# One GpSimd pass for the small inverses of two sequence mixers, with their matrix products planned together

## The chip, the cores and the metric

The kernel runs on one core of one Trainium2 chip. The metric is the device time of one launch in microseconds (us), the median of several runs; lower is better. A profiled execution of the same program gives a trace: every instruction of every engine with its start and duration. The engines are the matrix engine (TensorE, called PE in the profile), two elementwise engines (VectorE = DVE, ScalarE = ACT), GpSimd (POOL) and SyncE (SP), which here only issues DMA transfers.

## What is computed

One layer of a streaming encoder on a sequence of 512 tokens of width 2048, in float32:

```python
xn = rmsnorm(x); y = xn @ W_in               # 59 column blocks of 128
h  = x + concat[GDN(y_gdn), RWKV7(y_rwkv)] @ W_out
h  = h + cross_attention(rmsnorm(h), rmsnorm(mem))
h  = h + relu(rmsnorm(h) @ W_up)**2 @ W_down
out = rmsnorm(h)
```

GDN is a gated delta rule with 8 heads of 128, RWKV7 a state-space recurrence with 16 heads of 64. Both are causal recurrences that the kernel computes chunk by chunk. In both, each chunk of 64 tokens needs the inverse of a 64x64 triangular matrix (in the reference: `triangular_solve` in GDN, the step-by-step scan in RWKV7).

## The kernel before

**Stages.** (1) The input projection and both mixers run together: the 59 blocks of `y` are computed one after the other, and beside them, in 8 rounds, one RWKV column block (two heads of 64) and one GDN head per round. Block 3+7j to 9+7j belong to round j, in the order r, k, v of RWKV and k, q, v, z of GDN. (2) The keys of the attention (`kp`, `kq`), its values (`vp`, `vo`), the output projection (`op`), the scores (`sc`), the attention output (`at`). (3) The MLP: up in 32 units, down in 8, both by Strassen's seven products. Large products are done in fp32r, as three products of a split operand (`whi`, `wlo`, `xhi`, `xlo`); the small products of the mixers are plain fp32, which the trace shows as two passes each.

**Who sets the order.** Stage 1 is written as generators ("chains", L279 to 318), each yielding one instruction after the other. A planner inside the kernel (`run`, `start`, `cost`, `issue`, L211 to 318) keeps a modelled clock of each engine, and issues next the instruction that could start first. On TensorE equal starts go by rank: the mixers' chains (rank 3) ahead of the projections (rank 4). [...] So a mixer's small product runs as soon as the planner thinks its inputs ready, and the stream of `py` products fills all the rest. `cost` charges 100 ns for a change to another small tile shape and 120 ns for the first fp32r product after an fp32 one.

**A round of RWKV** (`rwkv`, L858 to 1081): decay (`pW`, `pA`, two Tanh, a scan, two Exp), key, normalisation, then the Gram matrices `GA`, `GB` by `pgA`, `pgB`; transposes and value products (`pk`, `pat`, `pv`, `pak`, `pkv`); the inverse; two levels that grow the 16x16 inverses to 64x64 (tiles `ri<j>x/w/s/t/u`); `pu`, `pwt`; eight state steps of two small products each (`rs`); the output (`po`, `pp`), its normalisation, and the store. The next round's chain starts after `pu`, `pwt` (L1029).

**A round of GDN** (`gdn`, L1092 to 1237): convolution and normalisation of the key, `pkk`, the masked matrix `NTm`; then the inverse, and beside it convolution of q and v, `pqk`, `pkt`, `pvt`; two levels (`gi<j>...`, six steps of small products); four state steps (`gs`), the output `gpo`, normalisation and store. The next round's chain starts at the very end (L1237).

**The inverses** (`inverse_blocks`, L767 to 806): the 64x64 matrices go to a DRAM tile (`nd`), come back as their 16x16 diagonal blocks, one block per partition; GpSimd runs 15 steps of two instructions on them; the result (T and its transpose U) goes through DRAM (`bg`) into the tiles where the levels read it. RWKV has 64 blocks a round, GDN 32; each has its own pass, and a list `solving` keeps the two passes from overlapping. Six loads bring T and U back for each mixer, issued on SP.

**Weight sums.** Strassen's products of the MLP's down weights need four sums of weight blocks per group (13 groups). Chains of low rank compute them on VectorE wherever there is room (`presum`, L400): four loads into `ds`, four subtractions or additions, four stores to DRAM (`sd`). What is not done in stage 1 is done during the MLP (`remaining`).

**The scores** (L1694 to 1727) are written without the planner: per step a load of 1024 columns, a split, 24 products.

## Time and profile before

| | us |
|---|---|
| median of 3 runs | 2889.58 |
| lowest and highest run | 2887.1, 2890.51 |
| span of the profiled execution | 2890.0 |
| TensorE busy, share of the span | 2862.2, 99% |
| VectorE busy | 2333.9, 81% |
| ScalarE busy | 1571.7, 54% |
| GpSimd busy | 214.7, 7% |
| stage 1 with the attention keys | 0 to about 1118 |

The span is the time from the first to the last instruction of that one execution. In the views of the trace a row of the timeline gives start, duration and the tiles (output<-inputs) of an instruction or of a run of like ones; the ends of matrix products are modelled, since they are pipelined, so the distance between two starts says more than a duration.

### The profile page before, as it was taken

How to read it: one execution, taken by the hardware profiler on the slowest of the kernel's cores; microseconds unless marked ns; L12 is line 12 of the kernel's file. 1: busy time of each engine (PE TensorE's matmuls, PEld its weight loads, DVE VectorE, ACT ScalarE, POOL GpSimd, SP SyncE). 2: the span in 40 equal slices, each digit the busy share in tenths (PEclk: the TensorE clock that was granted, in tenths of full speed). 3: DMA queues.
4: the chain of work that ended last, by engine and by line, in shares of the span. 5: the costliest groups of instructions: out<-in, count | busy, mean ns of one | idle time of the engine just before them, and what ended most of it. 6: DMA issues, size and time to landing. Idle time of an engine off the chain costs nothing.

```text
span 2890.0 us, 49168 instructions
## 1 busy us (share of the span) xinstructions
PE 2862.2 (99%) x18794; PEld 2419.1 (84%) x18794; DVE 2333.9 (81%) x3559; ACT 1571.7 (54%) x2233; POOL 214.7 (7%) x539
## 2 busy tenths in 40 slices
PE   9999999999999999999999999999999999999998
PEld 7877887877877888889988888888888888888887
DVE  7787787787877877769956898899998878786888
ACT  6555555645656655664445556555555644454544
POOL 0213213213212100000000000000000000000000
PEclk9999999999999999999999999999999999999999
DMA  5656656657656788784422354666565878887733
GB/s 191 166 147 176 176 149 187 165 154 189 180 161 200 214 257 274 232 292 151 124 95 88 110 164 153 199 195 207 189 200 178 292 249 277 295 257 247 265 101 110
DMA packets 321212, 553.01 MB, mean 191 GB/s; under 512 B 101128, under 2 KB 188428, under 8 KB 320976
## 3 DMA queue, kind: packets, MB, share of 16 engines
q1 hardware_dynamic: 293584, 518.41, 58.7%
q10 hardware_dynamic: 27392, 31.46, 3.1%
q8 instruction: 147, 2.41, 0.3%
q14 instruction: 89, 0.73, 0.1%
HBM read 443.45 MB, written 106.31 MB: 190 GB/s over the span
## 4 chain that ended last, share of the span: by engine, by line
PE 94%; DMA 3%; DVE 1%; ACT 1%; issue 1%; ACTq 0%; SPq 0%; DVEq 0%
PE py L257 22%; PE mxu L257 12%; PE mgd L257 6%; PE mgu L257 6%; PE mxd L257 6%; PE op L122 6%; PE vp L122 3%; PE mmu L257 3%; PE sc L122 3%; PE at L122 3%; PE scrd L257 3%; PE scgd L257 3%; PE mmd L257 3%; PE kq L257 3%; PE kp L257 2%; DMA wraw<-in_wo 1%
## 5 line engine op out<-in xcount | busy, mean ns | idle before, releaser
L257 ACT CAST whi<-wraw 128x1024 fp32r<-128x1024 f32 (+1 forms) x365 | 382.8, 1049 | 370.1 <-PE py L257 138.7
L257 DVE TENSOR_TENSOR wlo<-wraw,whi 128x1024 fp32r<-128x1024 f32 (+1 forms) x365 | 446.8, 1224 | 90.0 <-ACT whi L257 82.5
L257 PE MATMUL py<-xhi,whi 128*128 128x512 f32 x928 | 373.9, 403 | 6.8 <-ACT xhi L257 6.8
L257 PE MATMUL py<-xhi,wlo 128*128 128x512 f32 x928 | 373.1, 402 | 0.0
L257 PE MATMUL py<-xlo,whi 128*128 128x512 f32 x928 | 372.4, 401 | 0.0
L257 ACT CAST whi<-w 128x1024 fp32r<-128x1024 f32 x178 | 187.6, 1054 | 174.0 <-PE scgd L257 42.3
L257 DVE TENSOR_TENSOR wlo<-w,whi 128x1024 fp32r<-128x1024 f32 x178 | 217.3, 1221 | 43.4 <-ACT whi L257 40.9
L257 PE MATMUL mxu<-cb,whi 128*128 128x512 f32 x1016 | 249.3, 392 | 0.0
L257 PEld LDWEIGHTS mxu<-cb,whi 128*128 128x128 f32 x1016 | 184.7, 189 | 34.3
L257 PEld LDWEIGHTS py<-xhi,whi 128*128 128x128 f32 x928 | 175.3, 189 | 42.0 <-ACT xhi L257 6.8
L257 PEld LDWEIGHTS py<-xhi,wlo 128*128 128x128 f32 x928 | 175.3, 189 | 34.7 <-issue 1.0
L257 PEld LDWEIGHTS py<-xlo,whi 128*128 128x128 f32 x928 | 175.3, 189 | 33.8 <-DVE xlo L257 0.5
L131 DVE TENSOR_TENSOR wlo<-wraw,whi 128x1024 fp32r<-128x1024 f32 x112 | 136.7, 1222 | 44.8 <-ACT whi L130 44.3
L130 ACT CAST whi<-wraw 128x1024 fp32r<-128x1024 f32 x112 | 117.6, 1051 | 86.8 <-PE op L122 26.2
L257 PE MATMUL mxu<-cb,wlo 128*128 128x256 f32 x1016 | 142.7, 283 | 0.7 <-DVE wlo L257 0.7
L257 PEld LDWEIGHTS mxu<-cb,wlo 128*128 128x128 f32 x1016 | 135.1, 191 | 6.0 <-DVE wlo L257 0.9
L257 PE MATMUL mgu<-cb,whi 128*128 128x512 f32 x512 | 129.3, 394 | 0.1
L257 PE MATMUL mxd<-whi,cb 128*128 128x512 f32 x512 | 126.8, 389 | 0.0
L257 PE MATMUL mgd<-whi,cb 128*128 128x512 f32 x512 | 126.4, 389 | 0.0
L257 ACT ACT_TABLE_LOAD x87 | 111.6, 1283 | 16.5 <-DVE suml_gon L257 8.6
L122 PE MATMUL op<-ob,whi 128*128 128x256 f32 (+1 forms) x752 | 115.2, 304 | 0.0
L257 ACT CAST whi<-ws 128x1024 fp32r<-128x1024 f32 x75 | 79.0, 1053 | 64.0 <-PE mgu L257 48.1
(943 smaller groups left out, 6429.3 us busy)
## 6 DMA issues: line engine op xcount, KB each, us to landing
wraw<-in_w_in SPq DMA_DIRECT2D x116, 512.0 KB, 4.7
wraw<-in_w_up SPq DMA_DIRECT2D x65, 512.0 KB, 3.6
w<-in_w_up SPq DMA_DIRECT2D x63, 512.0 KB, 4.2
ds<-in_w_dm SPq DMA_DIRECT2D x128, 205.0 KB, 4.4
sd_s<-ds SPq DMA_DIRECT2D x128, 205.0 KB, 4.9
wraw<-sd_s SPq DMA_DIRECT2D x51, 512.0 KB, 4.9
w<-sd_s SPq DMA_DIRECT2D x50, 512.0 KB, 5.5
w<-in_w_dm SPq DMA_DIRECT2D x48, 512.0 KB, 4.9
```

What stands on the lines that cost most here:

```text
L122: PE.matmul(o, l, r, start=start, stop=stop, skip_group_check=again)
L130: S.copy(hi, src)
L131: V.tensor_tensor(out=lo, in0=src, in1=hi.bitcast(F32), op=ALU.subtract)
L257: f(*a, **k)
```

## The change

1. One pass on GpSimd per round for the blocks of both mixers: partitions 0 to 63 RWKV, 64 to 95 GDN. It starts when both matrices are stored. The writes of T and U of both come first, then RWKV's six loads, then GDN's six.
2. The planner adds 200 ns (`LEAVE`) to the start of an fp32r product while TensorE stands in fp32, so that another small product which could start within 200 ns goes first. It charges 190 ns instead of 100 for a change to another small shape, and 230 instead of 120 for the first fp32r product after a shape of fewer than 128 rows.
3. The decay part of RWKV's next round becomes a chain of its own (`decay`), released in the middle of the round before ("room"), and it must be drawn before the levels start. The key part of GDN becomes a chain of its own (`keys`), started after the inverse of the round before. GDN's next chain starts before the output's normalisation instead of after the store.
4. Some tiles take turns (`E2`/`v`, `tA`/`tB`), the scan is done in two halves with a shorter constant, GDN's state moves to another tile.
5. In the scores, every even step loads four blocks of down weights (512 columns) and every odd step sums and stores them: 8 pieces, two groups.
6. In the down projection's last unit one buffer is given back only after the sum that reads it.

The core of the diff:

```diff
-    CROSS = 150.0
+    CROSS, LEAVE = 150.0, 200.0
@@ cost
-                return n * 0.417 + (13.3 if state["shape"] is None else 120.0)
+                return n * 0.417 + (13.3 if state["shape"] is None else 120.0 if state["shape"][0] == P else 230.0)
-            sw = 0 if state["shape"] == sh or sh == (128, 128) else 100
+            sw = 0 if state["shape"] == sh or sh == (128, 128) else 190
@@ run
                 t = max(start(o) for o in c[3])
+                if c[3][0][0] == "PE" and state["shape"] is not None and c[3][0][6][0].dtype == F32R:
+                    t += LEAVE
@@ inverse_blocks
-    def inverse_blocks(nm, store, m, tags, temps, ready, out, moved=False):
-        np_ = 4 * m
...
-        yield lambda: not solving
-        solving.append(nm)
+    def inverse_blocks(j, tags, outs):
+        yield after("keys", j)
+        s1, s2 = tl("sgi"), tl("sgj", 240)
+        np_ = 96
...
-        yield SY.dma_start(D, blk)
+        rows_ = {"r": (slice(0, 64), 16), "g": (slice(64, 96), 8)}
+        for x in "rg":
+            yield after("stored", f"{x}i{j}")
+            yield SY.dma_start(D[rows_[x][0]], blks[f"{x}i{j}"])
...
+        for x in "rg":
+            r, m = rows_[x]
+            for t, b in (("T", Td), ("U", Ud)):
+                yield SY.dma_start(views(bg[m, t])[1], b[r])
+        for x in "rg":
+            r, m = rows_[x]
+            if x == "g":
+                yield after("gq", j)
...
+            events.add((f"{x}i", j))
@@ rwkv
+    def decay(j):
...
+        if j:
+            yield after("room", j)
         pW, pA = psb(f"pW{j}"), psb(f"pA{j}")
...
+        events.add(("drawn", j))
...
+        for s in (slice(0, 256), slice(256, 512)):
+            yield DV.tensor_tensor_scan(out=E2[:, s], data0=K("rst64"), data1=E2[:, s], initial=0.0,
+                                        op0=ALU.mult, op1=ALU.add)
...
+        events.add(("head", j))
+    def rwkv(j):
+        yield after("head", j)
+        tA, E1, E2 = heads.pop(j)
+        if j < 7:
+            chain(decay(j + 1), 3)
...
+        chain(stored(f"ri{j}", 16, store), 1)
+        chain(inverse_blocks(j, {"r": ("r", tE(j)), "g": ("gk", "gqn")}, outs), 1)
...
+        events.add(("room", j + 1))
...
         yield after("ri", j)
+        if j < 7:
+            yield after("drawn", j + 1)
@@ gdn
+    def keys(h):
...
+        fronts[h] = E, EG, eg, kn
+        events.add(("keys", h))
...
         events.add(("inverted", h))
-        vns, Ss = tl("gEs"), tl("gEG")
+        vns, Ss = tl("gEs"), tl("gqn")
+        if h < 7:
+            chain(keys(h + 1), 3)
...
+        if h < 7:
+            chain(gdn(h + 1), 3)
         o = tl("gkt")
...
-        if h < 7:
-            chain(gdn(h + 1), 3)
@@ scores
+    def fetched():
+        e, m, c, n = spans.pop(0)
...
+        for i in (A21, A22, A11, A12):
+            nc.sync.dma_start(b[i], I["w_dm"][e, m][i][:, c:n])
+    def summed():
+        e, m, c, n, (a11, a21, a22, a12) = held.pop()
+        for j, o, x, y, op in (("s1", a22, a21, a22, ALU.add), ("s3", a21, a11, a21, ALU.subtract),
+                               ("s2", a11, a22, a11, ALU.subtract), ("s4", a12, a12, a11, ALU.subtract)):
+            V.tensor_tensor(out=o, in0=x, in1=y, op=op)
+            nc.sync.dma_start(Sd[e, m, j][:, c:n], o)
...
             split(raw, wh, wl)
+            if n2 % 2 == 0:
+                fetched()
+            else:
+                summed()
```

## The prediction

> **What bounds the kernel now.** I read the page first, then who waits on the matrix engine, then its timeline inside one round, then the queues beside it. The page:

> ```profile
> span 2890.0 us, 49168 instructions
> PE 2862.2 (99%) x18794; PEld 2419.1 (84%) x18794; DVE 2333.9 (81%) x3559; ACT 1571.7 (54%) x2233; POOL 214.7 (7%) x539
> PEclk9999999999999999999999999999999999999999
> PE 94%; DMA 3%; DVE 1%; ACT 1%; issue 1%; ACTq 0%; SPq 0%; DVEq 0%
> ```

> TensorE is busy nearly all the time at full granted clock and carries 94% of the chain that ended last. Its waits on the mixers' state steps (the view of waits, all of them) are small:

> ```profile
> PE rs L257 <- DVE Qs L257: 2.2, 2, 1.2
> PE gs L257 <- DVE TtG L257: 1.2, 1, 1.2
> PE rs L257 <- DVE BK L257: 0.7, 1, 0.7
> ```

> So only fewer or shorter occupations of TensorE can save time. One of the steady rounds of the mixers, from the view by stretches (the second row counts the `py` products alone):

> ```profile
> 414.16:524.52 110.36, 110.36 (x1032) 88.48 (x1030) 86.88 (x165) 59.39 (x83) 26.40 (x66) 1.00 0.61 169
> 414.16:524.52 110.36, 87.25 (x337) 60.25 (x336) 4.84 (x7) 1.00 0.61 169
> ```

> A round is 110.4 us, and TensorE never idles in it; VectorE has 23 us to spare, GpSimd 84 us. (That a product's end is modelled makes the 87.25 us too large: by distance of starts, below, 337 `py` take 76.5 us.) The other 34 us are small products and what it costs to get to them and back. That cost is what the change works on, and the timeline shows it:

> ```profile
> 158.81 0.40 PE L257 MATMUL py<-xlo,whi 128*128 128x512 f32 x1
> 159.13 0.27 PE L257 MATMUL gi0x<-gk,gEs 64*64 64x64 f32 x2
> 159.53 0.50 PE L257 MATMUL py<-xhi,wlo 128*128 128x512 f32 x1
> 159.86 0.39 PE L257 MATMUL py<-xhi,whi 128*128 128x512 f32 x1
> ...
> 462.16 0.39 PE L257 MATMUL py<-xhi,wlo 128*128 128x512 f32 x1
> 462.39 0.39 PE L257 MATMUL py<-xhi,whi 128*128 128x512 f32 x1
> 462.71 0.27 PE L257 MATMUL ri3x<-r,GA 64*64 64x64 f32 x1
> 463.33 0.50 PE L257 MATMUL gn<-suml_gn,onesr 128*128 128x512 f32 x1
> 463.68 0.39 PE L257 MATMUL gn<-sumh_gn,onesr 128*128 128x512 f32 x1
> ...
> 478.80 0.39 PE L257 MATMUL py<-xlo,whi 128*128 128x512 f32 x1
> 479.03 0.33 PE L257 MATMUL rs<-BK,BTz 128*128 128x64 f32 x2
> 479.17 0.48 PE L257 MATMUL py<-xhi,wlo 128*128 128x512 f32 x1
> 479.48 0.40 PE L257 MATMUL py<-xhi,whi 128*128 128x512 f32 x1
> ```

> Undisturbed, big products start 0.23 us apart (462.16, 462.39). I call an interruption of that stream by fp32 products a visit, and price it by the starts around it. A GDN level (first block, 8 products in 16 passes): from 158.81 to 159.86 stand two big products and the visit, 1.05 - 2 x 0.227 = 0.60 us. A RWKV level (second block, 32 passes): 463.68 - 462.39 - 0.454 = 0.84 us. So 16 passes more cost 0.24 us, and a visit to 64-row shapes costs 0.60 - 0.24 = 0.36 us whatever is in it. A single state step (third block, full rows): 479.48 - 478.80 - 0.454 = 0.23 us for two passes. Two visits of 64-row products made into one save 0.36 us; two of full rows save less: the 0.23 us holds both passes, and what is fixed in it no row here parts; between 0 and 0.1 us, I take 0.05.

> **The change part by part.**

> *The pass on GpSimd.* Today's two passes of round 3, first and last instruction of each:

> ```profile
> 433.96 0.47 POOL L257 TENSOR_TENSOR sr<-sr 64x15 f32<-64x15 f32 x1 [18.52 <-DMA sr<-ndri]
> 449.22 0.62 POOL L257 COPY sr<-sr 64x256 f32<-64x256 f32 x1
> 468.43 0.41 POOL L257 TENSOR_TENSOR sgj<-sgi 32x15 f32<-32x15 f32 x1 [18.16 <-DMA sgi<-ndgi]
> 482.18 0.63 POOL L257 COPY sgi<-sgi 32x256 f32<-32x256 f32 x1
> ```

> 15.9 us for 64 partitions and 14.4 us for 32: the time hardly goes with partitions, so one pass of 96 costs about 16 us and 14 us of GpSimd go. Nothing waits for GpSimd but its own mixer, so that alone is worth nothing. What it does is to bring both results at one time. Today the levels stand apart (the chain, first two passes of each step; RWKV then GDN):

> ```profile
> 454.38 0.89 PE pkk L257 x8
> 462.78 0.20 PE ri3x L257 x2
> 465.88 0.20 PE ri3s L257 x2
> 469.24 0.20 PE ri3x L257 x2
> 471.46 0.20 PE ri3u L257 x2
> 474.11 0.20 PE pu L257 x2
> 491.60 0.20 PE gi3x L257 x2
> 494.26 0.20 PE gi3u L257 x2
> ```

> The common pass can start only after `pkk`, so RWKV waits for GDN: its levels move back by up to 29 us (462.8 to 491.6), less what the earlier key chain wins. Who waits for that? RWKV's output and the next `po`; the y buffers of the next round. The fifth eviction of that round, the first that needs a buffer of its own turn given back, stands at

> ```profile
> 546.49 0.69 DVE L257 TENSOR_TENSOR y<-py,rstd 128x512 f32<-128x512 f32 x1
> ```

> which is 43 us after levels that would end at about 503 (491.6 + the 11.3 us from `ri3x` to `pu` today). So the stream keeps running; the cover is those four buffers.

> *The shared visits.* Steps of RWKV's levels are 2.2 to 3.4 us apart, GDN's 2.7. A visit lasts 0.6 to 1.2 us and the planner now adds 0.2 us to it; a step of the other mixer falls into that with a probability of about 1.2/2.9, and the reverse case adds as much as 0.7/2.9: six in ten. Once two steps share a visit, the same VectorE delays follow for both, which favours the next. Against it: GDN's six loads come behind RWKV's six on SP, which took

> ```profile
> 453.20 1.72 SPq L257 DMA_DIRECT2D r<-bg16T  x2
> 454.96 3.77 SPq L257 DMA_DIRECT2D E<-bg16U  x4
> ```

> 5.5 us, so GDN starts one or two steps late and its last steps find no partner. Of six GDN steps I take four as shared: 4 x 0.36 = 1.44 us a round, 11.5 us in 8 rounds; the ends are none (0) and all (17.3).

> [...] The row of the single state step (128x128, 0.23 us with its passes) beside the GDN level (64x64, 0.36 us without them) says that the change of shape is the price. [...]

> ```profile
> 494.92 0.43 PE L257 MATMUL rs<-BK,BTz 128*128 128x64 f32 x2
> 495.29 0.33 PE L257 MATMUL gi3u<-gqn,gkn 64*64 64x64 f32 x4
> ```

> It occupies 0.37 us there against 0.23 alone. Today about one such case a round; with levels together and state steps together it goes, but `pqk` or `pkt` can take its place. I count 0, with 1.2 us (8 x 0.15) to either side. [...]

> *The hold.* The planner leaves fp32 only if nothing small can start within 0.2 us. There are 40 visits in a round by my count of the timeline, 320 in all. If one in five is held, for 0.1 us, that is 6.4 us, and full-row visits that join so give back some 0.05 us each and spare the stream a second visit; I take +2 us, between 0 and 24 (half of them held for 0.15 us).

> *Moved first parts.* `decay` and `keys` hold the same instructions as before (one scan becomes two halves, one instruction more a round on VectorE, inside its 23 us of room); their loads move on SP, which does not hold TensorE. `pW`, `pA` remain one visit. 0. The last rounds gain: GDN's levels and state steps no longer trail behind RWKV's, and of the waits above (2.2 + 1.2 + 0.7) I take 2 us as gone; 0 to 4, or as much lost to a new wait.

> *Weight sums in the scores.* The stretch of the scores:

> ```profile
> 1455.00:1545.00 90.00, 90.00 (x412) 74.73 (x411) 37.99 (x61) 32.85 (x54) 0.00 (x0) 1.00 0.31 98
> ```

> VectorE is busy 38 of 90 us. Eight pieces of four subtractions add 32 x 0.7 = 22 us (0.69 us for 512 columns, as the eviction above): it fits. The danger is SP: the stores wait for the sums, and the next step's load is queued behind them. A step is 24 products, 5.4 us; split, sums, load (my estimate: the split of 1024 columns 2.3, four sums 2.8, a load 4) take 9 us, but TensorE is up to three steps behind: 16 us. I take +0.5 us, 0 to 4. TensorE waits for no weight sum in the MLP, so taking them from there gains 0.

> *Sum*, against the profiled execution, whose span of 2890.0 is 0.4 us over the median of the runs, so that nothing lies around it: -11.5 + 0 + 2 - 2 + 0.5 = -11, which gives 2879 us.

> **The rivals.** (a) *Everything meets*: all six GDN steps share, and their passes overlap RWKV's. -17.3, and the serial last step (8 passes, 0.6 us) hides for about 0.4 us x 8 = 3.2; with -2 + 1: 2868.5. For it: common waits bind the chains. Against: the loads' 5.5 us. (b) *The chains miss each other*: one shared step a round, -2.9 + 2 - 2 + 0.5 = -2.4: 2887.6, no change to be seen. It is also the case in which the planner's order stays what it was. For it: 0.2 us is short against steps 2.7 us apart. (c) *The hold costs more than the visits*: TensorE stands in fp32 for a small product whose VectorE input comes late. At half of 320 visits and 0.15 us: 24 - 11.5 - 2 + 0.5 = +11, 2901 us. It decides from a mean of 0.04 us per visit (13/320) on, and is slower than measurable from 0.06. Against it: waits for VectorE are 4 us in all today, so the planner's clock is careful. (d) *A round runs out of buffers*: if levels end 43 us later than I think, `py` stops every round; some 20 us each, over 2900. The four y buffers speak against it.

> **How the numbers follow.** About 0.2% (5.8 us) is what a measurement of this kernel can tell from no change. Forecast 0.45; (a) 0.17, (b) 0.25, (c) 0.10, (d) 0.03. Faster: the forecast, (a), and a little of (b), 0.64; same: the rest of (b) and the weak end of the forecast, 0.24; slower: (c) and (d), 0.12. The range goes from beyond (a), 2865, to beyond (b), 2892, and leaves out (c) and (d).

> **What would show it.** Right: rounds of about 109 us instead of 110.4, `ri` and `gi` names inside one visit, one GpSimd pass of 96 partitions per round, some 36 visits a round, scores still about 90 us. Wrong: rounds of the old length with `gi` visits apart (b); idle time on TensorE in front of `rs`, `gs`, `ri` or `gi` (c); `py` waiting for an eviction (d); scores much over 91 us.

## The result, and the profile after

| | before | after |
|---|---|---|
| median of four runs each, us | 2890.05 | 2917.75 |
| lowest and highest | 2887.10, 2897.43 | 2915.83, 2928.06 |
| span of the profiled execution | 2890.0 | 2926.3 |
| first product of `kq` | 1022.3 | 1047.5 |
| first product of `vp` | 1118.2 | 1140.6 |
| scores, first `sc` to first `at` | 1455.3 to 1545.2: 89.9 | 1478.4 to 1581.5: 103.1 |
| from there to the end | 1344.8 | 1344.8 |

The ratio is 1.0101, with a 95% interval of 1.0079 to 1.0122: the kernel got 28 us slower, where 11 us less were forecast. The profiled execution after is the slowest of its four runs, 2928.06 us, 10.3 us above their median. The table says where the 36 us between the two spans lie: 22.4 us in the mixers and keys, 13.2 us in the scores, 0.7 between them, nothing behind them.

The page of the kernel after: total, busy time, and the chain that ended last.

```profile
span 2926.3 us, 48878 instructions
PE 2871.9 (98%) x18794; PEld 2432.9 (83%) x18794; DVE 2326.3 (79%) x3563; ACT 1565.6 (54%) x2231; POOL 126.2 (4%) x275
PE 87%; DMA 6%; DVE 2%; POOL 2%; issue 1%; ACT 1%; SPq 0%; ACTq 0%; POOLq 0%; DVEq 0%
```

TensorE runs the same 18794 products, but 54.4 us of its span are idle (2926.3 - 2871.9), against 27.8 before (2890.0 - 2862.2). For what it waited, says the view of waits (kernel after, the rows that are read below; total in us, times, longest):

```profile
PE ptr L1743 <- DVE plo L1746: 7.9, 1, 7.9
PE kp L257 <- ACT whi L257: 4.6, 1, 4.6
PE pwt L257 <- issue: 3.1, 1, 3.1
PE ri4u L257 <- issue: 3.1, 1, 3.1
PE rs L257 <- DVE Qs L257: 2.8, 1, 2.8
PE sc L122 <- DVE kql L131: 2.3, 1, 2.3
PE ri3u L257 <- issue: 1.5, 1, 1.5
PE ri2u L257 <- issue: 1.4, 1, 1.4
PE pu L257 <- issue: 0.7, 1, 0.7
```

Two things are new. In the scores TensorE waits for `plo` and `kql`, both written by VectorE. And in the mixers stand five waits, 9.8 us together, whose releaser is "issue": the profile shows nothing that TensorE waited for. Before had none of these. One of them in the timeline of TensorE (kernel after; start, duration):

```profile
624.40 0.22 PE L257 MATMUL ri4u<-E,k 64*64 64x64 f32 x2
...
625.04 0.22 PE L257 MATMUL ri4u<-E,k 64*64 64x64 f32 x2
628.32 0.37 PE L257 MATMUL ri4u<-E,k 64*64 64x64 f32 x2 [3.06 <-issue]
...
629.64 0.63 PE L257 MATMUL py<-xlo,whi 128*128 128x512 f32 x1
630.06 0.63 PE L257 MATMUL py<-xhi,wlo 128*128 128x512 f32 x1
```

In the middle of one tile's products TensorE stops for 3 us; then the big products start 0.42 us apart, not 0.23. The view by stretches names the second effect, the granted clock (seventh value behind the stretch):

```profile
628.00:634.40 6.40, 6.08 (x99) 4.82 (x100) 2.49 (x6) 2.79 (x7) 0.00 (x0) 0.50 0.39 124
```

Before `kq` the clock stands at one half for 30.7 us in five stretches after, and nowhere before. They begin at 177.2, 522.0, 627.8, 866.7 and 982.8 us and last 10.2, 3.4, 6.8, 3.4 and 6.8 us.

The half clock does not belong to the waits on "issue" alone. Two of the five stretches, 10.2 us, begin during such a wait or 1.7 us behind it (`ri4u`, `pwt`). The other three, 20.5 us, begin at or within 1 us of waits for VectorE (`rs` for `Qs`, 2.8 us; `gi3u` for `gkn`, 1.1 us) and for the weights of `kp` (4.6 us). Behind the wait of 1.4 us at `ri2u` the clock stayed full.

The signs the prediction named: GpSimd makes one pass of 96 partitions a round (the first and the sixth, kernel after), but five rounds take (719.43 - 150.33) / 5 = 113.8 us each, not 109.

```profile
150.33 0.63 POOL L257 COPY sgi<-sgi 96x256 f32<-96x256 f32 x1
719.43 0.61 POOL L257 COPY sgi<-sgi 96x256 f32<-96x256 f32 x1
```

`ri` and `gi` do share visits: by my count of the trace up to `kq`, 265 visits instead of 314. The visits did go; the time they should have freed was lost to new waits and to half clock. In TensorE's time up to `kq` (25.6 us more than before): waits +16.9 (24.5 us idle against 7.5), half clock on the big products +9.5, visits -0.8 though 49 fewer (some of them at half clock, which I put at 6 us of theirs).

### The profile page after: what moved, and what is told of

It is laid out like the page before. It is cut to its first block, busy times and chain, and to the rows that moved or that the text cites. A ratio compares the mean times of both kernels' runs of the same rounds, so it can differ in the third digit from the quotient of the medians.

```text
span 2926.3 us, 48878 instructions
## 1 busy us (share of the span) xinstructions
PE 2871.9 (98%) x18794; PEld 2432.9 (83%) x18794; DVE 2326.3 (79%) x3563; ACT 1565.6 (54%) x2231; POOL 126.2 (4%) x275
## 3 DMA queue, kind: packets, MB, share of 16 engines
q8 instruction: 147, 2.41, 0.3%
## 4 chain that ended last, share of the span: by engine, by line
PE 87%; DMA 6%; DVE 2%; POOL 2%; issue 1%; ACT 1%; SPq 0%; ACTq 0%; POOLq 0%; DVEq 0%
PE py L257 21%; PE mxu L257 12%; PE mgd L257 6%; PE mgu L257 6%; PE mxd L257 6%; PE op L122 5%; PE vp L122 3%; PE mmu L257 3%; PE at L122 3%; PE scrd L257 3%; PE scgd L257 3%; PE mmd L257 3%; PE kq L257 3%; PE kp L257 2%; DMA sd_s<-ds 1%
## 5 line engine op out<-in xcount | busy, mean ns | idle before, releaser
L257 ACT CAST whi<-wraw 128x1024 fp32r<-128x1024 f32 (+1 forms) x365 | 383.0, 1050 | 385.6 <-PE py L257 162.0
L257 DVE TENSOR_TENSOR wlo<-wraw,whi 128x1024 fp32r<-128x1024 f32 (+1 forms) x365 | 446.0, 1223 | 109.5 <-ACT whi L257 102.0
L257 PE MATMUL py<-xhi,whi 128*128 128x512 f32 x928 | 372.4, 401 | 6.9 <-ACT xhi L257 6.9
L257 PE MATMUL py<-xhi,wlo 128*128 128x512 f32 x928 | 375.1, 404 | 0.0
L257 PE MATMUL py<-xlo,whi 128*128 128x512 f32 x928 | 372.3, 401 | 0.3 <-DVE xlo L257 0.3
L257 ACT CAST whi<-w 128x1024 fp32r<-128x1024 f32 x178 | 187.6, 1054 | 172.8 <-PE scgd L257 42.3
L257 DVE TENSOR_TENSOR wlo<-w,whi 128x1024 fp32r<-128x1024 f32 x178 | 217.2, 1220 | 43.5 <-ACT whi L257 42.5
L257 PE MATMUL mxu<-cb,whi 128*128 128x512 f32 x1016 | 249.3, 392 | 0.0
L257 PEld LDWEIGHTS mxu<-cb,whi 128*128 128x128 f32 x1016 | 184.7, 189 | 34.3
L257 PEld LDWEIGHTS py<-xhi,whi 128*128 128x128 f32 x928 | 176.6, 190 | 43.6 <-ACT xhi L257 7.3
L257 PEld LDWEIGHTS py<-xlo,whi 128*128 128x128 f32 x928 | 176.5, 190 | 37.4 <-DVE xlo L257 1.3
L257 PEld LDWEIGHTS py<-xhi,wlo 128*128 128x128 f32 x928 | 176.2, 190 | 36.5 <-issue 1.8
L257 PE MATMUL mxu<-cb,wlo 128*128 128x256 f32 x1016 | 142.7, 283 | 0.7 <-DVE wlo L257 0.7
L257 PEld LDWEIGHTS mxu<-cb,wlo 128*128 128x128 f32 x1016 | 135.1, 191 | 6.0 <-DVE wlo L257 0.9
L257 PE MATMUL mgu<-cb,whi 128*128 128x512 f32 x512 | 129.4, 394 | 0.1
L257 PE MATMUL mxd<-whi,cb 128*128 128x512 f32 x512 | 126.8, 389 | 0.0
L257 PE MATMUL mgd<-whi,cb 128*128 128x512 f32 x512 | 126.4, 389 | 0.0
L257 ACT CAST whi<-ws 128x1024 fp32r<-128x1024 f32 x75 | 79.0, 1053 | 64.0 <-PE mgu L257 48.1
```

What stands on the lines that cost most here:

```text
L257: f(*a, **k)
```

## The experiments

Groups of weight sums are counted below, since they turned out to matter: before has 8.0 of 13 groups summed before the MLP, all beside the mixers and keys; after 6.2 there and 1.8 in the scores.

**The sums in the scores, taken away and put in alone.** `e1_no_sums` is the kernel after without `fetched` and `summed`; `e2_sums_only` is the kernel before with them.

```diff
-            if n2 % 2 == 0:
-                fetched()
-            else:
-                summed()
```

> The changed kernel without the weight sums in the scores (all else as changed; the sums not done there fall to the MLP again). Theory, sums: the pieces in the scores hold VectorE, which stands in front of the score's own work waiting for their loads; without them the scores take 90 us again (103 in the changed kernel's trace) and the kernel about 2905, +0.5% on before. Rival: the sums only moved, and their absence in the scores is paid in the MLP: scores 90, later stages longer by about as much, about 2917.

> The kernel before with nothing but the weight sums in the scores. Theory, sums: the loss in the scores needs no other part of the change: scores about 100 us, kernel about 2901, +0.4%. Rival: the scores only suffer because less was summed in the mixers or because TensorE was slow there after the mixers: 2890.

`e1_no_sums` took 2970.27 us (1.0267, 1.0252 to 1.0283), `e2_sums_only` 2902.80 (1.0039, 1.0024 to 1.0054). The second came as expected: the scores take 105.2 us there, and nothing is gained (10.0 groups are ready for the MLP, which with 8.0 waited for none). The first was missed by both theories. Its scores are back at 89.9 us, but the MLP now waits (view of waits, `e1_no_sums`):

```profile
PE scrd L257 <- ACT whi L257: 36.1, 2, 29.1
PE mxd L257 <- ACT whi L257: 21.1, 2, 20.2
```

57 us, because only 6.2 groups are ready. So the sums in the scores cost 13 us there and repair a loss of 57 that the rest of the change makes: its mixers leave less room for sums.

**The hold.** `e3_no_hold` is `e1_no_sums` without the 200 ns.

```diff
-    CROSS, LEAVE = 150.0, 200.0
+    CROSS, LEAVE = 150.0, 0.0
```

> The changed kernel without the weight sums in the scores and with the planner's hold at 0 instead of 0.2 us (new order throughout the mixers). Theory, hold: the mixers lose because TensorE is held for small products that come late; without it the mixers and keys end about 20 us earlier than in the same kernel with the hold, kernel about 2885. Theory, supply: they lose because long runs of tiny instructions outrun the fetch of TensorE's instructions (stalls with no releaser inside a run, then half the clock); shorter visits make those fewer, but GDN and RWKV still meet: 5 to 10 us, about 2897, and the waits that go are those without a releaser.

2950.49 us (1.0201, 1.0184 to 1.0218). `kq` starts no earlier without the hold, at 1054.5 us against 1039.3, and the waits on "issue" stay (10.5 us). So the hold does not cause them. (The total is lower than that of `e1_no_sums` because 6.6 groups are summed, and the MLP waits once, 26.4 us, instead of 57. Neither theory had this wait in its total, here and in the next run.)

**The levels kept apart.** `e4_apart` is `e1_no_sums` with GDN's levels held back until RWKV's `pu` and `pwt` are issued.

```diff
+        events.add(("grown", j))
@@ gdn
         yield after("gi", h)
+        yield after("grown", h)
```

> The changed kernel without the weight sums in the scores, and GDN's levels made to wait until RWKV's are done (after the products pu, pwt), so that the two mixers' levels share no visit. Theory, supply: no run of tiny instructions is longer than before, the stalls without a releaser are gone with the half clock behind them (25 us in the trace), and the visits that are no longer shared cost about 1.4 us a round back: about 2890. Theory, hold: the visits are as often held as before the edit; no change, about 2905.

2947.11 us (1.0191, 1.0176 to 1.0206). The waits on "issue" are nearly gone (0.8 us is the longest), so they come from the levels standing together. But the mixers are no faster: `kq` starts at 1047.1, with 23.9 us of half clock and other waits in their place (`e4_apart`):

```profile
PE pu L257 <- DVE v L257: 4.2, 2, 2.4
PE rs L257 <- DVE BK L257: 3.7, 2, 2.1
PE ri1x L257 <- DMA r<-bg16T: 2.9, 2, 2.6
```

**The planner's numbers alone.** `e5_planner_only` is the kernel before with part 2 of the change, as quoted in its diff.

> The kernel before with the planner's three numbers alone (hold 0.2 us, 190 and 230 ns for a change of shape): passes on GpSimd, chains and scores as before. Theory, supply: the hold is harmless by itself, since GDN's and RWKV's levels stay apart and no run of tiny instructions grows long; some 15 visits fewer, 3 to 5 us faster than before, about 2886, no stall without a releaser over 1 us. Rival, hold: TensorE is held in fp32 about 320 times; slower than before by 5 to 15 us, with waits in front of the small products.

2902.40 us (1.0038, 1.0026 to 1.0051), and 315 visits: with the chains unchanged, hold and prices join nothing. The time is that of the rival, 12.8 us above before. What the trace shows for it is, for the most part, two new waits, `PE ri6s` for `DVE k`, 9.3 us, behind a load of `memT` that VectorE's and ScalarE's fixed orders had put ahead, and `PE pkk` for `DVE gk`, 2.5 us, with 13.7 us of half clock at the two. Of the 15.4 us that the way from the first product to `kq` grew, idle time makes 7.6 and half clock in TensorE's work 3.6; in the 4.2 that are left short holds may stand. The planner's numbers changed the order, and the new order happens to be worse there; whether they cost as much in the kernel after is not shown.

**Dense products by themselves.** Why "issue"? The trace has a DMA queue of the kind `instruction` (page of the kernel after, queues):

```profile
q8 instruction: 147, 2.41, 0.3%
```

147 transfers of 16 KB (2.41 MB); the kernel before has as many. That they carry TensorE's instructions I read from their number: 18794 products and 18794 weight loads are 37588 instructions, 255.7 a transfer, and no other engine has a tenth of that. The five waits on "issue" fit this. In the order of all of TensorE's instructions in the trace (those of its sequencer counted too) they stand behind 2242, 6337, 8385, 10434 and 14785: 16, 8, 8 and 17 times 256 apart, to within one. So all five fall on a border of a block of 256. In the one shown above 519 instructions had run since the previous transfer began (611.75 us), and the next began at 625.34, when TensorE already stood; `pwt` is like it, with 510. In the other three the last transfer had begun 0.7 to 1.6 us before the stop. In all five TensorE went on 2.2 to 3.0 us after the start of the last transfer, which suggests that what it waited for came with it. So I put dense runs into the kernel before: `e6_burst_one` repeats the first level's products four more times in one run, in five rounds; `e7_burst_spread` does the same, each repetition only after eight more big products.

```diff
-            yield from pairs([pr(*x) for x in L4], [pr(*x) for x in H4])
+            for again in range(5 if l == 0 and 0 < j < 6 else 1):
+                yield from pairs([pr(*x) for x in L4], [pr(*x) for x in H4])
```

> The kernel before, in which rounds 1 to 5 repeat RWKV's first level products four more times, with the same result: 64 more products, 128 more passes, directly behind one another. The passes cost 128 x 0.0148 us x 5 rounds = 9.5 us, about 2901. Theory, supply: about 400 instructions of TensorE (passes and weight loads, with what precedes) in 3 us outrun their fetch, in most of the five rounds a stall without a releaser of 1 to 3 us inside the run and half the clock for 3.4 us or more behind it: 2910 to 2925. Rival, no limit: 2901 and no such stall.

> The control: the same 64 more products in rounds 1 to 5, but each repetition held back until eight more fp32r products have run, so in five visits instead of one. Both theories: the same passes, 9.5 us, and four more visits a round at 0.36 us, 7 us: about 2907. Theory, supply: no stall without a releaser, so less time than with the products in one run although there are 20 more visits. Rival, no limit: 7 us more than with the products in one run.

`e6_burst_one`: 2911.86 us (1.0072, 1.0057 to 1.0087), with seven waits as in the kernel after, 7.1 us together, all on borders of blocks. Half clock follows one of them alone (`ri4x`, 3.4 us). The three longest:

```profile
PE ri4x L257 <- issue: 1.8, 1, 1.8
PE ri1u L257 <- issue: 1.4, 1, 1.4
PE ri4w L257 <- issue: 1.1, 1, 1.1
```

`e7_burst_spread` has none over 0.2 us: the same products, spread, bring no such wait. So far the theory holds, for the waits. But it took 2931.78 us (1.0143, 1.0129 to 1.0157), 25 us more than expected: the chain of RWKV comes late, TensorE waits before `rs`, `gi7u` and `pv`, and the clock is halved for 19.8 us before `kq`. Spreading had a price of its own there, and so the times of the two runs don't decide between the theories; the waits do.

All fifteen traces together say how dense is dense. Up to `kq` they hold 1045 blocks and 46 waits on "issue" of over 0.4 us; 45 of the waits stand at a border (the other is `ri7t` in `e9_rate`, 0.5 us).

| the 256 instructions before the border took | blocks | of them with a wait behind |
|---|---|---|
| under 3 us | 8 | 2 |
| 3 to 4 us | 36 | 26 |
| 4 to 5 us | 49 | 10 |
| 5 to 6.1 us | 73 | 7 |
| over 6.1 us | 879 | 0 |

So in these traces such a wait stands only behind a block that ran in under 6.1 us, but a fast block does not decide it alone: the kernel before ran one block in 3.4 us without a wait, and the same mixers in `e2_sums_only` have one wait of 0.6 us. What makes one transfer start in time and another late is open. The time of 512 instructions, by which the next version limits the density, tells less: before three of the five waits of the kernel after the last 512 took 12.0 to 12.6 us, and its densest 512, 7.5 us, ended without one.

**A limit on the density, in the kernel after.** `e9_rate` puts a small product off while 512 instructions would have been planned in less than 13 us. In the kernel before the densest 512 take 11.4 us, after 7.5.

```diff
+                if c[3][0][0] == "PE" and c[3][0][6][0].dtype != F32R:
+                    t = max(t, past[-512] + RATE)
@@ issue
+            past.extend([t] * (2 if ins[0].dtype == F32R else 4))
+            del past[:-512]
```

> The changed kernel with one rule more in its planner: a small fp32 product is put off, and big products go first, as long as fewer than 13 us of planned time have passed since the 512th instruction of TensorE before it (a matrix product of fp32 counts as four instructions, one of fp32r as two); the pms product's py successor waits for one eviction more. Before, 512 instructions take 11.4 us in the densest place, in the changed kernel 7.5 us. By the planned order there are 315 visits where the changed kernel plans 306 and the kernel before 362, and TensorE's own work up to the scores comes to 1069 us against 1064 (changed) and 1077 (before). Supply theory: idle time of TensorE that nothing releases falls from 14 us to under 2 us in the mixers, the half clock there from 31 us to under 10, the keys (kq) start by 1035 us instead of 1047.5, the time is about 2904 us. Rival, late chains: products put off come late for VectorE, waits named by other engines take the place as in the run that kept the two mixers apart, and the time stays between 2912 and 2925 us.

2919.76 us (1.0095, 1.0078 to 1.0112): the rival. Of the waits on "issue" 2.5 us are left in two places, but `kq` starts at 1044.2. In their place (`e9_rate`, waits):

```profile
PE pu L257 <- DVE E L257: 6.9, 2, 4.6
PE kp L257 <- DVE wlo L257: 6.6, 1, 6.6
PE pu L257 <- DVE v L257: 3.2, 2, 2.5
```

This time VectorE's timeline tells why `E` was late (`e9_rate`):

```profile
177.00 1.82 DVE L257 TENSOR_TENSOR ds<-ds,ds 128x408 f32<-128x408 f32 x3 [8.12 <-DMA ds<-in_w_dm]
178.74 0.68 DVE L257 TENSOR_TENSOR y<-py,rstd 128x512 f32<-128x512 f32 x1
179.34 1.22 DVE L257 TENSOR_TENSOR wlo<-wraw,whi 128x1024 fp32r<-128x1024 f32 x1
180.47 0.68 DVE L257 TENSOR_TENSOR E<-E,ri0u 128x512 f32<-128x512 f32 x1
```

and TensorE's row beside it:

```profile
181.30 0.37 PE L257 MATMUL pu<-tA,E 64*64 64x64 f32 x2 [4.60 <-DVE E L257]
```

A weight sum (`ds`) stood 8.1 us at the head of VectorE's fixed order, waiting for its load; `E`, which TensorE needed, stood behind it, two more sums, `y` and `wlo`. VectorE kept that order although `E` could have been formed earlier: the last products of `ri0u` start at 172.97 us (TensorE, `e9_rate`), and VectorE ran nothing until 177.00. VectorE's waits for `ds` before `kq` are 21.0 us in `e9_rate`, 22.7 in `e4_apart`, 17.6 in `e3_no_hold`, but 3.9 before and 4.0 in the kernel after (4.0 to 9.3 in the five versions with its mixers): the versions that squeezed more sums into the changed mixers (7.0, 6.6 and 6.6 groups) paid for it.

**The scores.** Three versions of the kernel after, each against another reason for the wait at `plo`: smaller pieces in two sets of buffers, summed a step later (`e8_double_ds`); the next step's load issued on SP ahead of the sums' loads and stores (`e10_kq_ahead`); the sums written behind the step's products and transposes (`e11_sums_behind`).

```diff
@@ e8_double_ds
-        b = [pl.tile([P, 512], F32, tag=f"ds{i}", name=f"ds{e}_{m}_{c}_{i}", bufs=1)[:, 0:n - c] for i in range(4)]
+        b = [pl.tile([P, 256], F32, tag=f"ds{i}", name=f"ds{e}_{m}_{c}_{i}", bufs=2)[:, 0:n - c] for i in range(4)]
@@ e10_kq_ahead
             split(raw, wh, wl)
+            if want:
+                kqload()
             if n2 % 2 == 0:
@@ e11_sums_behind
             if g == 1 and n2 == 3:
                 turned()
+            if n2 % 2 == 0:
+                fetched()
+            else:
+                summed()
```

> The changed kernel with its pieces in the scores halved (256 columns) and in two sets of buffers, each summed one step after its load was issued; the same columns but for rounding. Theory, sums: VectorE loses its time in the scores because a load waits for the stores of the piece before and the sum for that load; with two sets nothing waits, the scores take 90 to 92 us instead of 103, about 2907 against 2918 of the changed kernel. Rival: the amount of work on VectorE or SP is too much for the scores: still about 100 us.

> The changed kernel, with the load of the scores' next 1024 columns issued on SP one step earlier, ahead of the weight sums' loads and stores; all else is the same, and the mixers are. Queue theory: in the scores it is SP's order that costs, since the next step's load stands behind four stores that wait for the sums; then the scores take about 92 us instead of 103, and the time is about 2907 us. Rival, VectorE's order: plo and kql still stand behind sums that wait for their loads; then the scores keep more than 99 us and the time stays within 4 us of 2918.

> The changed kernel, with the loads and sums of the weights in the scores put behind the step's products and behind the transposes of the probabilities, where they stood ahead of both. VectorE's order theory: the 7.9 us in front of ptr and the 2.3 us in front of sc go with the half clock after them, the scores take about 91 us and the time is about 2907 us. Rival, queue on SP: the next step's load still stands behind the stores; the scores keep 98 us or more and the time is above 2912 us.

None helped: 2916.62 us (1.0094, 1.0069 to 1.0118), 2924.33 (1.0109, 1.0088 to 1.0130) and 2927.98 (1.0131, 1.0116 to 1.0146), with scores of 100.2, 104.9 and 107.2 us. The waits in front of `ptr` were 5.3, 8.2 and 8.1 us. So neither the buffers nor SP's order decide by themselves. `e11_sums_behind` did not test what it was meant to, and its trace says so: VectorE's order in it is not that of the text. The sums written behind the transposes still run ahead of `plo` (VectorE, `e11_sums_behind`):

```profile
1553.69 2.14 DVE L1762 TENSOR_TENSOR ds<-ds,ds 128x512 f32<-128x512 f32 x3 [3.75 <-DMA ds<-in_w_dm]
1557.40 0.69 DVE L1762 TENSOR_TENSOR ds<-ds,ds 128x512 f32<-128x512 f32 x1 [1.56 <-DMA ds<-in_w_dm]
1558.01 1.22 DVE L131 TENSOR_TENSOR kql<-kqr,kqh 128x1024 fp32r<-128x1024 f32 x1
1559.14 1.28 DVE L1746 TENSOR_TENSOR plo<-ptr,phi 128x512 fp32r<-128x512 f32 x2
```

The kernel after has the same order:

```profile
1552.58 0.69 DVE L1762 TENSOR_TENSOR ds<-ds,ds 128x512 f32<-128x512 f32 x1 [2.71 <-DMA ds<-in_w_dm]
1554.46 1.42 DVE L1762 TENSOR_TENSOR ds<-ds,ds 128x512 f32<-128x512 f32 x2 [1.19 <-DMA ds<-in_w_dm]
1556.80 0.69 DVE L1762 TENSOR_TENSOR ds<-ds,ds 128x512 f32<-128x512 f32 x1 [0.92 <-DMA ds<-in_w_dm]
1557.41 1.22 DVE L131 TENSOR_TENSOR kql<-kqr,kqh 128x1024 fp32r<-128x1024 f32 x1
1558.55 1.28 DVE L1746 TENSOR_TENSOR plo<-ptr,phi 128x512 fp32r<-128x512 f32 x2
```

The two transposes that wait need a bank that `plo` gives back (the wait of 7.9 us at `ptr` ended with it), and `plo` is queued behind the splits of later steps and the sums between them. That left one explanation for both stages: weight sums that wait for their loads, ahead of what TensorE needs, in VectorE's fixed order.

**That explanation, in each stage by itself.** `e12_late_sums` is `e9_rate` with the planner told that the loads of `ds` land later, so that the sums take a later place (5.4 groups instead of 7.0). `e13_first_half` is `e9_rate` with sums only in the first eight of the sixteen steps of the scores, far from the transposes (one group instead of two).

```diff
@@ e12_late_sums
-                yield from presum(e, m, c, min(c + width, 2048), d, Lane(nc.sync, "SP", margin=5000.0), Lane(nc.sync, "SP", 0.0, 0.0))
+                yield from presum(e, m, c, min(c + width, 2048), d, Lane(nc.sync, "SP", margin=10000.0), Lane(nc.sync, "SP", 0.0, 0.0))
@@ e13_first_half
-            if n2 % 2 == 0:
+            if g == 0 and n2 % 2 == 0:
                 fetched()
-            else:
+            elif g == 0:
                 summed()
```

> The kernel of the rate limit, with one number more changed: the planner takes the loads of the weight sums to land 10 us later than it models, not 5, and so places the sums later in VectorE's order and finds room for fewer (5.4 groups in the mixers against 7.0; 1.6 more in the scores, as before). Theory, sums in VectorE's order: with the rate limit the three long waits of TensorE (pu, 10.1 us in all) stand right behind stretches in which VectorE waited 8.1, 3.6 and 4.5 us for a load of ds; VectorE's waits for ds before the scores fall from 21 us to under 6, those of pu to under 2 us, the keys (kq) start by 1032 us instead of 1044. Rival, the levels are late for themselves (TensorE gets their products too late): pu keeps more than 6 us and kq starts at 1040 or later. The total, by the first theory about 2907 us without a wait for the sums in the MLP, about 2933 with one of 26 us as in the runs of 6.6 groups; the second is the likelier here.

> The kernel of the rate limit, with weight sums only in the first half of the scores' steps (4 pieces, one group, instead of 8 pieces); no sum stands any more between the transposes of the probabilities and their evictions in VectorE's order. Theory, sums in VectorE's order: the 9 us in front of ptr and the half clock behind it go, the scores take at most 95 us instead of 101.6, the time is about 2911 us. Rival, each piece has its price wherever it stands (12 us by 8): the scores take about 96 to 98 us with a wait in front of sc instead of ptr, and the time is 2913 us or more.

`e13_first_half`: 2905.07 us (1.0047, 1.0030 to 1.0063). The scores take 89.9 us, as before, at full clock, without any wait: four pieces cost nothing there. The version halves the number of pieces as well as moving them away from the transposes. But in the kernel after, too, TensorE waits for nothing in the first 67.5 us of the scores, some 12 of the 16 steps (1478.4 to 1545.9); so it is the last pieces that cost, not each piece. The view by stretches, `e13_first_half` and then the kernel after:

```profile
1465.90:1555.50 89.60, 89.60 (x409) 74.38 (x408) 47.26 (x75) 32.36 (x54) 0.00 (x0) 1.00 0.55 177
```

```profile
1478.40:1581.30 102.90, 92.73 (x410) 76.27 (x409) 55.19 (x92) 32.53 (x54) 0.00 (x0) 0.93 0.69 220
```

`e12_late_sums`: 2948.15 us (1.0193, 1.0178 to 1.0209). Its mixers answer the question: VectorE waits 0.5 us for `ds`, TensorE no longer for `pu`, and `kq` starts at 1032.3. The three longest waits that remain (the first product apart), `e12_late_sums`:

```profile
PE scrd L257 <- ACT whi L257: 27.4, 1, 27.4
PE ptr L1749 <- DVE plo L1752: 9.5, 1, 9.5
PE kp L257 <- ACT whi L257: 5.9, 1, 5.9
```

The first row is the bill for too few sums (7.25 groups), as expected, though the total is 15 us above the 2933 that went with it; the second is the scores' wait, whose sums this kernel kept.

One caution for all the times of `kq`: the mixers of the kernel after, `e1_no_sums`, `e8_double_ds`, `e10_kq_ahead` and `e11_sums_behind` have the same order on VectorE and ScalarE, and their five profiled executions reach `kq` at 1047.5, 1039.3, 1040.5, 1032.9 and 1044.1 us, with 30.7, 20.5, 20.5, 10.2 and 20.5 us of half clock before it. The mixers of before, with `e2_sums_only`, reach it at 1022.3 and 1020.8. So the 1032.3 of `e12_late_sums` is no proof of speed by itself, and the 22.4 us of the table above belong to the slowest of five; what `e12_late_sums` shows is that the `pu` waits are gone. Every version with the changed mixers stays above before.

## Why the prediction was wrong, step by step

**What bounds the kernel**: right. TensorE is 87% of the chain, and all of the loss is idle time or half clock of TensorE.

**The pass on GpSimd**: "worth nothing" in itself, right; it takes 17.5 us (477.18 to 494.71), not 16. What was missed is on SP. The writes of the common result wait for GpSimd at the head of SP's queue (the last step on GpSimd ends at 974.49 us), and the weights of `kp` are queued behind them (SP and ScalarE, kernel after):

```profile
974.51 0.59 SPq L257 DMA_DIRECT2D bg16T<-sgi  x1
...
978.00 0.36 SPq L257 DMA_DIRECT2D wraw<-in_wk  x1
```

```profile
982.53 1.04 ACT L257 CAST whi<-wraw 128x1024 fp32r<-128x1024 f32 x1 [9.94 <-DMA wraw<-in_wk]
```

Between 967.9 and 974.5 us SP issued nothing; ScalarE waited 9.9 us, TensorE 4.6 (the `kp` row of the waits). The prediction looked at GDN's loads behind RWKV's on SP and not at what else stands behind the writes. This reading is argued from the rows; no run removed it.

**The shared visits** (-11.5): a step that failed in size, by about half. The price was right: a fit over the visits of the trace at full clock (fixed part and price per pass) gives about 0.3 us for a visit that holds 64x64 products, before and after, against 0.36. The number was not: visits that hold 64x64 products fell from 111 to 92, 19 and not 32. And the other 30 visits that went were of full rows, whose fixed part in the fit is close to nothing: over visits of full rows alone 0.02 us before and 0.01 after, beside 0.11 us a pass (the prediction took 0.05). 19 x 0.31 = 6 us, which is about what the sum of all visits shows once half clock is taken out (-0.8 - 6).

**State steps between products of 64 rows**: 0 was taken, from the row of `rs` at 494.92 inside a GDN visit (0.37 us against 0.23 alone), and about 0 came. Changes between 64 and 128 rows inside a visit cost about 0.1 us each in the fit, and there are 37 before and 33 after: -0.4 us by this estimate. No run takes such changes by themselves.

**The hold** (+2): its size is not measured by itself; the 4.2 us left over in `e5_planner_only` are the most that the runs allow for short holds there. Without it the changed mixers were no faster (`e3_no_hold`); with the prices, in the kernel before, it went with 12.8 us more (`e5_planner_only`), through two long waits that the new order brought. Rival (c) gave a slower time, 2901, and `e5_planner_only` took 2902; but the rival's reason, many short holds, can make at most a third of that run's loss.

**Moved first parts** (tail -2): wrong sign. The last wait of `kp` grew from 2.7 to 4.6 us and `pvt` waits 2.6 us more.

**Weight sums in the scores** (+0.5, 0 to 4): wrong, +13. The prediction gave VectorE's sum of busy times (it fits: 55 of 103 us) and looked for the danger on SP (its estimate of a load, 4 us, is near the median of the `ds` loads on the page of before, 4.4). The place that counts is the order on VectorE: the sums that waited 2.7, 1.2 and 0.9 us for their loads in the rows above held back what stood behind them, `kql` and `plo` among it; the wait at `plo` is 7.9 us, that at `kql` 2.3 us, and the half clock around the first (1549.4 to 1563.0 in the trace, 5.8 us of it outside the wait, worth 2.9) makes the rest. `e13_first_half` shows it: without the pieces near the transposes the price is 0. Also wrong: "TensorE waits for no weight sum in the MLP, so taking them from there gains 0". That holds while enough groups are done: 7.8 were enough (`e5_planner_only`, `e6_burst_one`, `e7_burst_spread`: 1344.8 us from `at` to the end, as before). The changed mixers leave room for 6.2, and the runs with 6.2 to 7.25 groups paid 26 to 57 us. Why the planner finds less room is open; no run isolated it.

**What no step had**: waits of TensorE at the borders of its instruction blocks. The prediction counted what dense small products save and not what they need. The term of idle time in its sum, waits of TensorE before `kq`, was -2 us; +16.9 came, 9.8 of it on "issue", and the half clock beside it. Behind 36 of the 85 blocks that ran in 3 to 5 us such a wait stands, and I put it down to transfers that came late; 10.2 of the 30.7 us of half clock stand at these waits. That dense products bring them was shown by making them in the kernel before (`e6_burst_one`, 7.1 us) and by nearly removing them from the changed kernel in two ways (`e4_apart`, 1.0 us; `e9_rate`, 2.5 us). Removing them did not make the kernel faster, though, and so the density is a cause of the waits, but not by itself of the 22 us: with them gone, a chain that gave up its dense place came late elsewhere. In `e9_rate` that was the sums' order on VectorE; with that gone too (`e12_late_sums`) about 10 us stay between its `kq` and that of before: from the first product on 9.0, of which idle time makes +5.3, half clock in TensorE's work +8.7 (half of 17.5), and the rest, the visits among it, -5.0. What keeps the clock down there once the long waits are gone is open: one stretch (508 to 512 us) follows a wait of 1.4 us on "issue"; another (853 to 863) lies where TensorE had no `py` to run between 847.9 and 854.2 us, probably for the limit's extra wait for one eviction.

No version beat the kernel before. The nearest with the changed mixers, `e13_first_half`, is 0.47% slower; of those with the mixers of before, the planner's numbers alone cost 0.38% and the sums in the scores alone 0.39%.

## What to carry to other kernels

Before packing small products more densely, count instructions as well as time: here no block of 256 instructions of TensorE that took over 6.1 us had a wait on "issue" behind it, and of those that took 3 to 4 us most had (0 of 879, and 26 of 36). On an engine that keeps its order, as VectorE did here, filler work that waited for a load was not free, for all the room in the busy share: VectorE was busy 55 of 103 us in the scores, and TensorE waited 7.9 us for `plo` behind the sums. Look at what stands behind the filler, in the order the trace shows and not the one the text has. And a wait of 1 to 3 us on TensorE could cost more than its length here: the one of 3.1 us at `ri4u` went with 6.8 us of half clock, that of 3.1 us at `pwt` with 3.4, that of 1.4 us at `ri2u` with none (kernel after).

- Waits of TensorE with no releaser, up to 3.5 us long (3.1 in the kernel after), stand at borders of blocks of 256 of its instructions and end 2.2 to 3.3 us after a transfer of 16 KB begins (147 of them, 2.41 MB). Of 1045 borders 45 have one of over 0.4 us, all behind a block that ran in under 6.1 us.
- The clock was halved for 3.4 us after a wait of only 1.4 us (`e12_late_sums`, 508 us), inside a stretch of small products; after an equal wait in the kernel after (`ri2u`, 405 us) it was not.
- The fit gives an fp32 visit of full rows a fixed price of 0.02 us before and 0.01 after, a visit with 64x64 products one of about 0.3 us.
